# The norms' sums, spread and last stores of a one-core encoder trunk, rearranged

## The chip, the core and the metric

The kernel runs on one core of one Trainium2 chip. Such a core has five engines with a queue of instructions each: TensorE (PE, matrix products; its weight loads are listed as PEld), VectorE (DVE), ScalarE (ACT), GpSimd (POOL) and SyncE (SP), which here issues the DMA transfers. The metric is the device time of one execution, in microseconds (us). The kernel before the change was timed three times, and one more execution was profiled.

## The reference

One layer of a hybrid encoder on 2048 positions of width 1024, in float32, closed by a norm:

```python
def rmsnorm(x, w):
    xf = x.astype(jnp.float32)
    y = xf * lax.rsqrt(jnp.mean(xf * xf, axis=-1, keepdims=True) + EPS)
    return (y * w.astype(jnp.float32)).astype(x.dtype)

def hybrid_layer(x, ...):
    h = rmsnorm(x, norm_mix_w)
    proj = jnp.einsum("btd,dc->btc", h, w_in)
    u_b, u_c, u_h, z, xbc, dt_raw = jnp.split(proj, SPLITS, axis=-1)
    y_a = short_conv_mixer(u_b, u_c, u_h, short_conv_w)
    y_b = ssd_mixer(z, xbc, dt_raw, ssd_conv_w, ssd_conv_b, dt_bias, a_log, d_skip, ssd_norm_w)
    y = jnp.concatenate([y_a, y_b], axis=-1)
    x = x + jnp.einsum("btc,cd->btd", y, w_out)
    h = rmsnorm(x, norm_mlp_w)
    hid = jnp.square(jax.nn.relu(jnp.einsum("btd,df->btf", h, w_up)))
    return x + jnp.einsum("btf,fd->btd", hid, w_down)
...
    return rmsnorm(x, final_norm_w)
```

What matters here is `rmsnorm`: a sum of squares over the 1024 features of each position, a root, and a scaling of all features of that position by its result.

## The kernel before

Activations lie transposed: the 1024 features are eight tiles of 128 partitions, and positions run along the free dimension, in blocks of 512 (`TB`). So a sum over features is a sum over eight tiles and over the 128 partitions. Large products are made of three products of split operands (a high and a low fp32r part each, `mm3`, lines 112 to 114, and the chain at lines 269 to 271). Positions are worked through in two halves of two blocks; the half's two blocks share products in a scheme of seven instead of eight.

The class `Rstd` makes a norm in steps. The eight squares (ScalarE) are added into one tile, `acc`, on VectorE. `reduce` sums that tile over the partitions on PE: with 128 positions at a time as the stationary operand and a column of ones as the moving one, so that `pst` holds a position on each partition and a column for each 128 of them (line 131, fp32). `root` takes the root on ScalarE (line 143) and the reciprocal on VectorE (144), splits the result into two fp32r parts (146, 147), and multiplies the identity by each (`diag`, line 151). `spread` multiplies a matrix of ones by the two diagonal tiles (line 177, fp32r), which puts each position's factor on all partitions, in `prb`; ScalarE copies that to SBUF (line 180). `reduce`, `root` and `spread` serve the first two blocks' norms (`begin_block`, lines 471 to 474), at the very start of the program, where PE has nothing else to do for the first of them, and the three parts of the last norm. The norms between use other functions of the class (`parts`, `whole`), which the change leaves alone.

The program's end is `rest` (line 1025 on): the last products of the second MLP product for the second half, a few features (d) at a time, added to what was accumulated, and with each finished tile its square. It goes through three parts: the third block of 512 positions whole, then the last block in two parts of 256. Each part's norm (`norm_out`, a generator) is advanced by `step()` once ahead of every tile's products of the part that follows, and to its end after the last part. The last square of a part isn't added to `acc` on VectorE: `reduce` sums it on PE beside `acc` (two products per column). Then each of the eight tiles is scaled by its weight and by the factor: five on VectorE in one instruction that reads `prb` (line 1084), three (k = 1, 4, 7) on ScalarE by the weight (1081) and then on GpSimd by the copied factor (1082). SyncE stores each tile (line 1087).

The order on each engine's queue is not the written one throughout: a scheduler places the instructions by the order of writing and its own estimates, and an engine then works through its queue strictly in order.

## Time and profile before

| what | us |
|---|---|
| three runs | 2643.14, 2642.49, 2636.65 |
| their median | 2642.49 |
| the profiled execution's own time | 2640.53 |
| its span, first to last instruction | 2638.80 |
| PE busy | 2588.8 (98%) |
| VectorE busy | 1955.7 (74%) |
| ScalarE busy | 1432.9 (54%) |
| GpSimd busy | 58.2 (2%) |

Times in the profile run from the span's start. A row of the timeline is: start in us, length in us, engine, line, operation, written tile <- read tiles, shapes, the number of instructions (consecutive ones of a kind are merged), and in brackets the idle time of the engine ahead of it with what ended it. A row of the waits is: engine, tile and line that waited, engine, tile and line that ended the wait; the sum in us, the number of times, the longest. An fp32 product shows as two instructions, an fp32r one as one.

### The profile page before, as it was taken

The page shows a single profiled execution, that of the slowest core. Times are in us where ns is not written, and L with a number is a line of the kernel's source. Part 1 is how long each engine was busy: PE and PEld are TensorE (multiplying, and loading weights), DVE is VectorE, ACT ScalarE, POOL GpSimd, SP SyncE. Part 2 cuts the span into 40 slices and gives each one's busy share as a digit, 9 for nine tenths or more (in the row PEclk, how much of TensorE's full clock was granted, in tenths as well). Part 3 has the DMA queues.
Part 4 walks back from the last instruction along what each step waited for, and adds up shares of the span by engine and source line. Part 5 has one row for each costly group of instructions (what it writes and reads, how often), then busy time and mean ns, then how long its engine had stood idle before and what let it go on. Part 6 is the DMA issues. An engine that isn't in the chain of part 4 may idle for free.

```text
span 2638.8 us, 33504 instructions
## 1 busy us (share of the span) xinstructions
PE 2588.8 (98%) x12034; PEld 2127.0 (81%) x12034; DVE 1955.7 (74%) x2696; ACT 1432.9 (54%) x2175; POOL 58.2 (2%) x98
## 2 busy tenths in 40 slices
PE   7999999999999999999999999999999999999998
PEld 5778888788888888888888888788887888888777
DVE  7987676777777777778767765755558877888885
ACT  6644345777667666666326555655555444444443
POOL 0000010000000000000000000000000000000001
PEclk9999999999999999999999999999999999999999
DMA  3585344655555578977665674744448554665762
GB/s 146 190 302 191 137 151 168 207 162 163 171 160 183 154 253 266 283 221 224 211 210 211 232 271 140 261 158 140 161 148 294 165 150 150 214 210 180 238 202 72
DMA packets 283718, 511.25 MB, mean 194 GB/s; under 512 B 25248, under 2 KB 139936, under 8 KB 283552
## 3 DMA queue, kind: packets, MB, share of 16 engines
q1 hardware_dynamic: 283552, 509.12, 58.6%
q8 instruction: 94, 1.54, 0.2%
q14 instruction: 72, 0.59, 0.1%
HBM read 343.88 MB, written 165.15 MB: 193 GB/s over the span
## 4 chain that ended last, share of the span: by engine, by line
PE 65%; issue 25%; DMA 4%; DVE 3%; ACT 3%; SPq 0%; POOL 0%; POOLq 0%; DVEq 0%; ACTq 0%
PE px L269 9%; PE px L271 9%; PE px L270 9%; PE py L269 5%; PE py L271 4%; PE py L270 4%; PE pm L112 4%; PE pm L113 4%; PE pm L114 4%; PE pw L269 2%; PE pw L271 2%; PE pw L270 2%; DMA dec<-rd_d 1%; PE yd L1280 1%; PE yo L1277 1%
## 5 line engine op out<-in xcount | busy, mean ns | idle before, releaser
L269 PE MATMUL px<-uh,whi 128*128 128x512 f32 x1672 | 656.9, 393 | 10.3 <-ACT pw L277 5.6
L271 PE MATMUL px<-uh,wlo 128*128 128x512 f32 x1672 | 651.4, 390 | 2.6 <-DVE wlo L104 2.6
L270 PE MATMUL px<-ul,whi 128*128 128x512 f32 x1672 | 651.9, 390 | 0.0
L269 PEld LDWEIGHTS px<-uh,whi 128*128 128x128 f32 x1672 | 314.1, 188 | 84.7 <-ACT pw L277 8.1
L104 DVE TENSOR_TENSOR wlo<-wraw,whi 128x1024 fp32r<-128x1024 f32 x230 | 233.2, 1014 | 197.9 <-ACT whi L103 197.8
L271 PEld LDWEIGHTS px<-uh,wlo 128*128 128x128 f32 x1672 | 314.3, 188 | 69.5 <-DVE wlo L104 3.4
L270 PEld LDWEIGHTS px<-ul,whi 128*128 128x128 f32 x1672 | 314.4, 188 | 63.8
L103 ACT CAST whi<-wraw 128x1024 fp32r<-128x1024 f32 x230 | 203.5, 885 | 283.3 <-PE px L270 192.1
L103 ACT CAST whi<-s 128x1024 fp32r<-128x1024 f32 x210 | 219.6, 1046 | 233.1 <-PE py L270 76.1
L269 PE MATMUL py<-uh,whi 128*128 128x512 f32 x836 | 326.9, 391 | 2.3 <-DVE acc L986 1.9
L270 PE MATMUL py<-ul,whi 128*128 128x512 f32 x836 | 325.5, 389 | 0.0
L271 PE MATMUL py<-uh,wlo 128*128 128x512 f32 x836 | 325.3, 389 | 0.0
L104 DVE TENSOR_TENSOR wlo<-s,whi 128x1024 fp32r<-128x1024 f32 x210 | 255.2, 1215 | 88.9 <-ACT whi L103 87.0
L112 PE MATMUL pm<-uh,whi 128*128 128x512 f32 (+1 forms) x648 | 252.0, 390 | 2.1 <-ACT uh L204 2.1
L114 PE MATMUL pm<-uh,wlo 128*128 128x512 f32 (+1 forms) x648 | 248.3, 383 | 0.0
L113 PE MATMUL pm<-ul,whi 128*128 128x512 f32 (+1 forms) x648 | 248.3, 383 | 0.0
L269 PEld LDWEIGHTS py<-uh,whi 128*128 128x128 f32 x836 | 156.9, 188 | 35.9 <-DVE acc L986 2.3
L271 PEld LDWEIGHTS py<-uh,wlo 128*128 128x128 f32 x836 | 156.9, 188 | 32.8
L270 PEld LDWEIGHTS py<-ul,whi 128*128 128x128 f32 x836 | 157.0, 188 | 32.2
L269 PE MATMUL pw<-uh,whi 128*128 128x512 f32 x418 | 163.4, 391 | 0.7 <-ACT pw L277 0.7
L319 ACT CAST uh<-rh 128x1024 fp32r<-128x1024 f32 (+1 forms) x128 | 120.4, 944 | 79.1 <-PE py L271 64.4
L271 PE MATMUL pw<-uh,wlo 128*128 128x512 f32 x418 | 162.9, 390 | 0.0
(233 smaller groups left out, 3750.3 us busy)
## 6 DMA issues: line engine op xcount, KB each, us to landing
hid_d<-e SPq DMA_DIRECT2D x96, 512.0 KB, 3.9
rh<-hid_d SPq DMA_DIRECT2D x96, 512.0 KB, 4.4
wraw<-w_in SPq DMA_DIRECT2D x68, 512.0 KB, 4.2
wraw<-w_up SPq DMA_DIRECT2D x64, 512.0 KB, 4.3
wraw<-w_down SPq DMA_DIRECT2D x104, 256.0 KB, 3.7
dec<-rd_d SPq DMA_DIRECT2D x32, 512.0 KB, 5.7
wraw<-w_out SPq DMA_DIRECT2D x32, 512.0 KB, 5.1
x_d<-xt SPq DMA_DIRECT2D x64, 256.0 KB, 3.9
```

The lines of the kernel that those rows point to most:

```text
L103: nc.scalar.copy(hi, raw)
L104: eng.tensor_tensor(out=lo, in0=raw, in1=hi.bitcast(F32), op=ALU.subtract)
L112: nc.tensor.matmul(out, whi, hi, start=(k == 0), stop=False)
L113: nc.tensor.matmul(out, whi, lo, start=False, stop=False)
L114: nc.tensor.matmul(out, wlo, hi, start=False, stop=(k == nk - 1))
L269: nc.tensor.matmul(p, hi, h[0], start=bool(first and k == 0), stop=False, **kw)
L270: nc.tensor.matmul(p, hi, h[1], start=False, stop=False, **kw)
L271: nc.tensor.matmul(p, lo, h[0], start=False, stop=(k == len(g) - 1), **kw)
L319: nc.scalar.copy(p[i][0], t)
L1277: nc.tensor.matmul(yo[:, j * L : (j + 1) * L], state[:, j * P : (j + 1) * P], cT, start=True, stop=True)
L1280: nc.tensor.matmul(yd[(i % 2) * 64 : (i % 2) * 64 + 64, (i // 2) * L : (i // 2 + 1) * L], byhead(t["xdt"])[:, i, :], t["dec"][:, i, :], st ...
```

## The change

Four edits. *The sums:* `reduce` goes through its tiles in the outer loop and through the columns in the inner one. In the last part alone (`final`) the last three squares, not one, are left out of VectorE's sum and given to `reduce`: eight products, the two on `acc` first and the two on the last square at the end. *Root and spread:* the split into two parts is gone, in all norms that use `root`; one diagonal tile in fp32, one fp32 product in place of two fp32r ones. *The scalings:* the tiles of GpSimd are 1, 4 and 5, and ScalarE's scaling by the weight stands right behind the root, ahead of the spread. During the last part's first four tiles `step()` is called twice per tile, and not during its last two. *The stores:* in the last part tiles 1, 3, 4 and 5 are stored by ScalarE's queue, the others by SyncE's.

```diff
--- before.py
+++ after.py
@@ -126,14 +126,15 @@
 
         def reduce(self, *accs):
             pst = psum("tp", "pst", 2)
-            for c in range(self.n):
-                for i, acc in enumerate(accs):
+            for i, acc in enumerate(accs):
+                for c in range(self.n):
                     nc.tensor.matmul(
                         pst[:, c : c + 1],
                         acc[:, c * P : (c + 1) * P],
                         ones[:, 0:1],
-                        start=(i == 0),
+                        start=(i + c == 0),
                         stop=(i == len(accs) - 1),
+                        skip_group_check=True,
                     )
             self.sums = pst[:, 0 : self.n]
 
@@ -142,19 +143,13 @@
             r = self.pool.tile([P, n], F32, tag="rs", name="rs", bufs=2)
             nc.scalar.activation(r, self.sums, AF.Sqrt, bias=eps, scale=self.scale)
             nc.vector.reciprocal(out=r, in_=r)
-            r2 = self.pool.tile([P, 2, n], F32R, tag="rs2", name="rs2", bufs=2)
-            nc.vector.tensor_copy(r2[:, 0, :], r)
-            nc.vector.tensor_tensor(out=r2[:, 1, :], in0=r, in1=r2[:, 0, :].bitcast(F32), op=ALU.subtract)
-            self.diag = []
-            for i in range(2):
-                diag = self.tmp("diag")[:, 0 : self.w].bitcast(F32R)
-                nc.vector.tensor_tensor(
-                    out=diag.rearrange("p (c t) -> p c t", c=n),
-                    in0=ident.unsqueeze(1).to_broadcast([P, n, P]),
-                    in1=r2[:, i, :].bitcast(F32).unsqueeze(2).to_broadcast([P, n, P]),
-                    op=ALU.mult,
-                )
-                self.diag.append(diag)
+            self.diag = self.tmp("diag")[:, 0 : self.w]
+            nc.vector.tensor_tensor(
+                out=self.diag.rearrange("p (c t) -> p c t", c=n),
+                in0=ident.unsqueeze(1).to_broadcast([P, n, P]),
+                in1=r.unsqueeze(2).to_broadcast([P, n, P]),
+                op=ALU.mult,
+            )
 
         def parts(self, acc):
 
@@ -173,8 +168,7 @@
 
         def spread(self, rb=None):
             prb = self.ps = psum("tp", "prb", 2)[:, 0 : self.w]
-            for i in range(2):
-                nc.tensor.matmul(prb, ones_r, self.diag[i], start=(i == 0), stop=(i == 1))
+            nc.tensor.matmul(prb, ones, self.diag, start=True, stop=True)
             if rb is None:
                 rb = self.pool.tile([P, TB], F32, tag="rstd", name="rstd", bufs=1)[:, 0 : self.w]
             nc.scalar.copy(rb, prb)
@@ -1037,6 +1031,7 @@
             sums = [self.dp.tile([P, TB], F32, tag="acc", name="facc", bufs=18) for _ in range(NBB)]
             for bb, t0, w in ((0, 0, TB), (1, 0, TB // 2), (1, TB // 2, TB // 2)):
                 ts = slice(t0, t0 + w)
+                final = t0 > 0
                 st = self.rstd(w)
                 acc = sums[bb][:, ts]
 
@@ -1049,12 +1044,14 @@
 
                 square(0, True)
                 square(4)
+                apart = []
                 for (d, fs, blocks), (whi, wlo) in ws:
                     for i in range(2):
                         at = [(b, j) for b, blk in enumerate(blocks) for j in range(2) if blk == 2 * i + j]
                         if not at:
                             continue
-                        step()
+                        for _ in range(1 + final if d < 3 else 1 - final):
+                            step()
                         pm = psum("mm", "pm", 4)[:, 0:w]
                         todo = [(b * len(fs) + k, j, f) for b, j in at for k, f in enumerate(fs)]
                         for n, (c, j, f) in enumerate(todo):
@@ -1064,27 +1061,36 @@
                             mm3(pm, whi[:, cs], wlo[:, cs], hi, lo, n, len(todo))
                         o = tiles[d + 4 * i, bb][:, ts]
                         nc.vector.tensor_tensor(out=o, in0=pm, in1=o, op=ALU.add)
-                        sq = square(d + 4 * i, False, (d, i) == (3, 1))
-                tails.append(self.norm_out(tiles, bb, ts, st, acc, sq))
+                        alone = (d, i) in (((2, 1), (3, 0), (3, 1)) if final else ((3, 1),))
+                        sq = square(d + 4 * i, False, alone)
+                        if alone:
+                            apart.append(sq)
+                if final:
+                    st.reduce(acc, *apart)
+                tails.append(self.norm_out(tiles, bb, ts, st, final, acc, *apart))
             while tails:
                 step()
 
-        def norm_out(self, tiles, bb, ts, st, *sums):
-            st.reduce(*sums)
+        def norm_out(self, tiles, bb, ts, st, final, *sums):
+            if not final:
+                st.reduce(*sums)
             st.root()
+            slow = (1, 4, 5)
+            for k in slow:
+                nc.scalar.mul(tiles[k, bb][:, ts], tiles[k, bb][:, ts], col(C_NFIN, k))
             yield
             r = st.spread()
             yield
             for k in range(KD):
                 o = tiles[k, bb][:, ts]
-                if k % 3 == 1:
-                    nc.scalar.mul(o, o, col(C_NFIN, k))
+                if k in slow:
                     nc.gpsimd.tensor_tensor(out=o, in0=o, in1=r, op=ALU.mult)
                 else:
                     nc.vector.scalar_tensor_tensor(
                         out=o, in0=o, scalar=col(C_NFIN, k), in1=st.ps, op0=ALU.mult, op1=ALU.mult
                     )
-                nc.sync.dma_start(out[NBB + bb, :, k, ts], o)
+                queue = nc.scalar if final and k in (1, 3, 4, 5) else nc.sync
+                queue.dma_start(out[NBB + bb, :, k, ts], o)
                 if k % 2:
                     yield
```

The line numbers shift: 1047 becomes 1042, 1066 becomes 1063, 1084 becomes 1089, 177 becomes 171. On VectorE, the end of the queue before (sums of squares 1047, tiles picked up from PSUM 1066, scalings of the second part 1084, then the root):

```order
L1066 TENSOR_TENSOR acc<-pm,acc 128x256
L1047 TENSOR_TENSOR facc<-facc,sq 128x256
L1084 SCALAR_TENSOR_TENSOR acc<-acc,cv,prb 128x256
L1047 TENSOR_TENSOR facc<-facc,sq 128x256
L1066 TENSOR_TENSOR acc<-pm,acc 128x256
L1084 SCALAR_TENSOR_TENSOR acc<-acc,cv,prb 128x256
L144 RECIPROCAL rs<-rs 128x2
L146 CAST rs_21862<-rs 128x2
L147 TENSOR_TENSOR rs_21862<-rs,rs_21862 128x2
L151 TENSOR_TENSOR diag<-ident,rs_21862 128x256 x2
L1084 SCALAR_TENSOR_TENSOR acc<-acc,cv,prb 128x256 x5
```

and in the changed program:

```order
L1042 TENSOR_TENSOR facc<-facc,sq 128x256
L1063 TENSOR_TENSOR acc<-pm,acc 128x256
L1089 SCALAR_TENSOR_TENSOR acc<-acc,cv,prb 128x256 x2
L1042 TENSOR_TENSOR facc<-facc,sq 128x256
L1063 TENSOR_TENSOR acc<-pm,acc 128x256 x3
L145 RECIPROCAL rs<-rs 128x2
L147 TENSOR_TENSOR diag<-ident,rs 128x256
L1089 SCALAR_TENSOR_TENSOR acc<-acc,cv,prb 128x256 x5
```

The last three tiles are now picked up one behind the other, with the second part's scalings and all sums of squares ahead of them. On PE, where the second part's norm lies among the last part's products, before:

```order
L114 MATMUL pm<-uh_21439,wlo 128x256
L131 MATMUL pst<-ones_r,facc 128x1
L112 MATMUL pm<-uh_21445,whi 128x256
L113 MATMUL pm<-ul_21446,whi 128x256
L114 MATMUL pm<-uh_21445,wlo 128x256
L112 MATMUL pm<-uh_21451,whi 128x256
L113 MATMUL pm<-ul_21452,whi 128x256
L114 MATMUL pm<-uh_21451,wlo 128x256
L112 MATMUL pm<-uh_20986,whi 128x256
L131 MATMUL pst<-ones_r,sq 128x1
L131 MATMUL pst<-ones_r,facc 128x1
L131 MATMUL pst<-ones_r,sq 128x1
```

and now:

```order
L112 MATMUL pm<-uh_21272,whi 128x256
L131 MATMUL pst<-ones_r,facc 128x1 x2
L113 MATMUL pm<-ul_21273,whi 128x256
L114 MATMUL pm<-uh_21272,wlo 128x256
L112 MATMUL pm<-uh_21427,whi 128x256
L113 MATMUL pm<-ul_21428,whi 128x256
L114 MATMUL pm<-uh_21427,wlo 128x256
L112 MATMUL pm<-uh_21433,whi 128x256
L131 MATMUL pst<-ones_r,sq 128x1 x2
```

Counted in products of 256 columns from the second part's first, `pst` starts after 88 of them (93 before) and `prb` of this norm stands after 104 (118 before, its second product after 120); the first part's `prb` stands after 25 (32 and 35 before). The last part's `pst` and `prb` still follow the last product, number 144. On ScalarE, at the program's start (casts of weights 103, then the first block's copy of `prb` and the second block's first square):

```order
L103 CAST whi<-wraw 128x1024 x2
L180 COPY facc<-prb 128x512
L464 ACTIVATE facc<-x_212 128x512
L204 CAST uh_248<-x_182 128x512
L464 ACTIVATE sq<-x_212 128x512
```

and now:

```order
L103 CAST whi<-wraw 128x1024 x2
L458 ACTIVATE facc<-x_212 128x512
L174 COPY facc<-prb 128x512
L198 CAST uh_242<-x_182 128x512
L198 CAST uh_251<-x_182 128x512
```

The square stands ahead of the copy now. Smaller moves of this kind run through the queues of PE, VectorE, ScalarE and SyncE up to about PE's 800th product; from there to the last parts all queues read as before. At ScalarE's end the four stores are its last instructions, behind the last copy of `prb`.

## The prediction

> **What bounds the kernel now.** I read the page's shares first, then TensorE's waits at both ends of the program, then the timeline of the last 14 us.
>
> ```profile
> PE 2588.8 (98%) x12034; PEld 2127.0 (81%) x12034; DVE 1955.7 (74%) x2696; ACT 1432.9 (54%) x2175; POOL 58.2 (2%) x98
> ```
>
> PE is the bound nearly everywhere, so only three places can pay: the start, where PE has nothing to do, the work added to or taken from PE itself, and the end, after its last large matmul. The waits of PE, first for 0 to 250 us (the first four rows), then from 2400 us on (the last three):
>
> ```profile
> PE pst L131 <- DVE facc L469: 12.9, 1, 12.9
> PE px L271 <- DVE wlo L104: 2.6, 2, 1.5
> PE pm L112 <- ACT uh L204: 2.1, 1, 2.1
> PE prb L177 <- DVE diag L151: 1.6, 1, 1.6
> ...
> PE pst L131 <- DVE facc L1047: 1.6, 1, 1.6
> PE prb L177 <- DVE diag L151: 1.3, 1, 1.3
> PE pst L131 <- ACT sq L1045: 0.5, 1, 0.5
> ```
>
> The edited norm stands in both groups: pst and prb are its two steps on PE. The end, engine by engine:
>
> ```profile
> 2617.96 0.28 PE L114 MATMUL pm<-uh,wlo 128*128 128x256 f32 x1
> 2618.39 0.38 PE L131 MATMUL pst<-ones_r,facc 128*128 128x1 f32 x2
> 2625.69 0.28 PE L113 MATMUL pm<-ul,whi 128*128 128x256 f32 x1
> 2625.81 0.28 PE L114 MATMUL pm<-uh,wlo 128*128 128x256 f32 x1
> 2627.51 0.41 DVE L1066 TENSOR_TENSOR acc<-pm,acc 128x256 f32<-128x256 f32 x1
> 2628.01 0.42 ACT L1045 ACTIVATE sq<-acc 128x256 f32<-128x256 f32 x1 [1.04 <-DVE acc L1066]
> 2628.48 0.38 PE L131 MATMUL pst<-ones_r,sq 128*128 128x1 f32 x2 [0.46 <-ACT sq L1045]
> 2628.95 0.36 PE L131 MATMUL pst<-ones_r,sq 128*128 128x1 f32 x2
> 2629.35 0.26 ACT L143 ACTIVATE rs<-pst,cv 128x2 f32<-128x2 f32 x1 [0.38 <-PE pst L131]
> 2629.64 0.17 DVE L144 RECIPROCAL rs<-rs 128x2 f32<-128x2 f32 x1 [1.34 <-ACT rs L143]
> 2629.84 0.17 DVE L146 CAST rs<-rs 128x2 fp32r<-128x2 f32 x1
> 2630.12 0.75 DVE L151 TENSOR_TENSOR diag<-ident,rs 128x256 fp32r<-128x256 f32 x2
> 2630.59 0.72 PE L177 MATMUL prb<-diag,ones_r 128*128 128x256 f32 x2 [1.28 <-DVE diag L151]
> 2631.81 2.05 DVE L1084 SCALAR_TENSOR_TENSOR acc<-acc,cv,prb 128x256 f32<-128x256 f32 x5 [0.94 <-ACT rstd L180]
> 2631.85 2.09 POOL L1082 TENSOR_TENSOR acc<-acc,rstd 128x256 f32<-128x256 f32 x3 [5.78 <-ACT rstd L180]
> 2632.60 0.33 SPq L1087 DMA_DIRECT2D out<-acc  x1
> 2635.96 0.40 SPq L1087 DMA_DIRECT2D out<-acc  x1
> ```
>
> From PE's last product (done 2626.09) to the span's end at 2638.80 are 12.7 us in three pieces: VectorE picks the product up 1.42 us late, because its queue holds older work; sum, root and spread run from 2627.51 to 2631.81 (call that moment D); then eight stores leave SyncE one by one, the last 2 us after its data were ready (2633.94).
>
> **The change part by part.** *VectorE's backlog.* Of the last part's squares two are no longer added on VectorE (2 x 0.41, by the 256-wide DVE row), and cast, subtraction and one of two diag products go in each norm: 0.17 + 0.16 + 0.65 with four columns, about 0.7 with two. That is some 2.5 us less between the first and last norm, against a backlog of 1.42. In the new order the scalings of the part ahead all stand before the last three pick-ups, which follow each other directly; PE needs six products, 0.12 apart (2625.69 to 2625.81), for each of these tiles, so 0.72, and VectorE 0.41: it has time. Bounds: 0 if other waits keep VectorE late, 1.42 if it is level with PE. I take -1.42, since the work removed is nearly twice the backlog.
>
> *Sums after the last square.* Today three pst products follow it (2628.48 to 2629.31, 0.83 us, one of them on facc). With the order turned, six of eight are done before, and two remain: 0.24 to the second, and 0.36, so 0.60: -0.23.
>
> *Root and spread.* Today reciprocal to the end of prb takes 1.67 (2629.64 to 2631.31). Then: 0.20 to the diag product, 0.47 from its start to prb's (2630.12 to 2630.59), and one fp32 product instead of two fp32r ones. No wide fp32 product of this norm is in the trace; its price comes from these:
>
> ```profile
> 1033.33 1.05 PE L1277 MATMUL yo<-bc,state 128*128 128x128 f32 x8
> 1035.89 0.39 PE L113 MATMUL pm<-ul,whi 128*128 128x512 f32 x1
> 1036.12 0.39 PE L114 MATMUL pm<-uh,wlo 128*128 128x512 f32 x1
> ```
>
> Four fp32 products of 128 columns show as eight instructions; less a drain of 0.16 (0.39 long, 0.23 apart) that is 0.11 each, so 0.22 per 128 columns, 0.44 for 256, 0.89 for 512. An fp32r one of 512 takes 0.23. So the last spread is 0.44 + 0.2 drain = 0.65, the chain 1.32: -0.35 (bounds -0.45 and 0, the latter if an fp32 product cost twice that).
>
> *PE ahead of the end.* The two earlier spreads of the last norm cost 0.89 + 0.44, against two fp32r products each, 0.46 + 0.23: +0.64. Against that stand pauses, such as the 0.31 before the second part's pst (2618.39, where 2618.08 was free), which go if VectorE is less late. Between 0 and +0.64: I take +0.3. So D comes 1.7 earlier against the span's start, if nothing moved there.
>
> *Stores.* Here are all 24 issues (min/median/max ns) and the rate per 1 us slice, 2600 to 2640 us:
>
> ```profile
> L1087 SPq DMA_DIRECT2D out<-acc x24: 332/396/2009, 2613.3 to 2636.0; - x24
> DMA to landing us min/median/max: 1.7/1.9/3.8
> GB/s 0 0 0 0 0 8 0 0 0 0 0 0 0 16 246 6 285 375 381 377 383 53 0 0 0 178 264 264 211 131 0 0 0 150 267 268 269 94 0 0
> ```
>
> The last eight leave D+0.79 to D+4.15, 0.48 apart; 128 KB in 0.48 us is the 267 to 269 GB/s of their slices, while the 256 KB stores of the first part reached 380. So issuing is the limit. With two queues of four, the last tile is ready at D+2.13 (POOL's third), leaves 0.32 later (as the first does after its data) at D+2.45 and lands 1.9 later: D+4.35 against D+6.05, a gain of 1.7. But eight tiles at 380 GB/s need 0.345 each: the first lands at D+2.69, the last then at D+5.1, a gain of 0.95. I take -1.3 between. No DMA is issued by ScalarE in this trace; with the price of SyncE's median 0.40 its four issues fit, with the maximum 2.0 they don't (a rival below). Nothing is queued behind them on ScalarE. The scalings moved ahead of the spread on ScalarE were early already, and cost nothing: ScalarE is idle 1 us and more between the squares.
>
> [...]
>
> *The start.* Both norms of the first stage use the same code:
>
> ```profile
> 15.09 0.18 DVE L144 RECIPROCAL rs<-rs 128x4 f32<-128x4 f32 x1 [1.12 <-ACT rs L143]
> 15.59 1.29 DVE L151 TENSOR_TENSOR diag<-ident,rs 128x512 fp32r<-128x512 f32 x2
> 16.32 1.40 PE L177 MATMUL prb<-diag,ones_r 128*128 128x512 f32 x2 [1.57 <-DVE diag L151]
> 17.76 0.58 ACT L180 COPY facc<-prb 128x512 f32<-128x512 f32 x1 [0.82 <-PE prb L177]
> 18.25 0.63 ACT L464 ACTIVATE facc<-x 128x512 f32<-128x512 f32 x1
> 19.84 1.65 PE L112 MATMUL pm<-uh,whi 128*128 128x512 f32 x3 [2.11 <-ACT uh L204]
> 22.99 0.63 PE L113 MATMUL pm<-ul,whi 128*128 128x512 f32 x1
> 23.41 0.48 PE L114 MATMUL pm<-uh,wlo 128*128 128x512 f32 x1
> ```
>
> Here PE works at half pace: 0.42 apart (22.99 to 23.41) instead of 0.23. The diag product starts 0.20 after the reciprocal, prb 0.73 after that, at 16.03; 0.89 x 0.42/0.23 = 1.63 and a drain of 0.2 end it at 17.9, against 17.72: +0.2. The square that now stands ahead of the copy on ScalarE takes 0.63, and the engine is idle for 0.82 before the copy, so it is hidden if its input has landed. The second norm, on a busy PE, costs 0.89 - 0.46 = +0.43. Sum: +0.6. The order of all engines changes over the first 200 us or so; PE's largest wait there after its first product, 2.6 us for wlo, may shrink or grow. I take 0 for that, between -2 and +2.
>
> **Sum:** -1.42 - 0.23 - 0.35 + 0.3 - 1.3 = -3.0 at the end, +0.6 at the start: -2.4. The profiled execution took 2640.53 (span 2638.80): 2638.1. It lies 0.2 below the mean of the three runs (2640.76), which scatter from 2636.65 to 2643.14; I forecast 2638.4 for the median, the mean less 2.4.
>
> **The rivals.** (1) *The stores gain nothing*, landing as late as before: -1.1, 2639.7. For it: transfers near 380 GB/s; against it: the 267 of today. (2) *PE waits for the moved sums.* In the second part pst stands five products earlier and prb fourteen; if VectorE keeps its backlog, PE stalls there about as long as its present waits by facc and diag at the very end, 1.6 + 1.3 halved, and the 1.42 is not won: -2.4 + 1.45 + 1.42 = +0.5, 2641.2. Against it: the 2.5 us taken from VectorE. (3) *The half pace at the start ends earlier.* It lasts from 19.84 to about 23.4, where a product gets shorter. The longer product at 16.0 keeps PE busy before; were the 3.6 us halved, 1.8 x (1 - 0.23/0.42) = 0.8 would be won; with the start's waits 2 us shorter as well, -5.2: 2635.6. (4) *Slower: ScalarE issues dearly.* Place: the four stores after the last spread. First issue at D+1.06 (POOL's first at D+0.74, and 0.32), last at D+1.06+3c. D is 1.7 earlier, the start 0.6 later, so it is slower than today from 1.06 + 3c = 4.15 + 1.1, c = 1.4 us on. At the maximum of 2.0 the last leaves at D+7.06: +1.8, 2642.6. For it: no row of ScalarE issuing; against it: 0.40 as SyncE's median.
>
> [...]
>
> **How the numbers follow.** Chances: the forecast 0.62, (1) 0.13, (2) 0.12, (3) 0.08, (4) 0.05. All lie within 5.2 us, and 0.3% (about what a measurement of this kernel can tell from no change) is 7.9 us, so only the scatter of runs, 6.5 us wide, can carry the median past it: faster 0.11 (runs like 2636.65 less 2.4 give 2634.25, past 2634.6), same 0.86, slower 0.03. The range goes from the fast run with rival (3)'s half, 2633.5 (2636.65 - 2.4 - 0.8), to the slowest run with rival (2)'s +0.5, 2643.6.
>
> **What would show it.** Right: the last pick-up on VectorE starts within 0.2 us of PE's last product; 0.6 us of pst after the last square; one prb of two rows, 0.65 long; D to the span's end 5.3 to 6.1 instead of 7.0; the first pm product near 20.0. Wrong: store issues on ScalarE of over a microsecond, new waits of PE for facc, sq or diag in the last 20 us, or a first 250 us that shifts by more than 2 us.

## Result and profile after

| | before | after |
|---|---|---|
| median of 16 runs each, us | 2640.18 | 2635.31 |
| ratio of the times, 95% interval | | 0.9982 (0.9975 to 0.9989) |
| profiled execution: own time, us | 2640.53 | 2634.66 |
| its span, us | 2638.80 | 2632.33 |

The kernel is 0.18% faster, 4.9 us by the medians: less than the 0.3% that the prediction took as the limit of what can be told from no change, and twice the 2.4 us forecast. One of the change's 16 runs was a slow one of 3721.07 us, at a granted clock of 0.655; the ratio leaves it out, and without it the median is 2635.02. The spans of the two profiled executions differ by 6.47 us. (The time outside the span is 1.73 us before and 2.33 after, which no stretch shows.) I cut both spans at four moments: the first pm product, the start of the 600th of the px, py and pw products (the input projection, at about 220 us; counted from 0), the first of the 144 pm products that are 256 wide (the last block's two parts), and the end of PE's last large product, T.

| stretch, us | before | after | difference |
|---|---|---|---|
| start to first pm | 19.84 | 19.96 | +0.1 |
| first pm to 600th product | 200.56 | 197.41 | -3.1 |
| 600th product to the last block's parts | 2384.0 | 2383.0 | -1.0 |
| those parts, to T | 21.69 | 21.92 | +0.2 |
| T to the end | 12.71 | 10.02 | -2.7 |

The third row is scatter, as the experiments show. So the end gave nearly what was forecast, -2.5 (the last two rows) where -3.0 was expected, and the first 220 us, forecast at +0.6, came out at -3.0.

PE's share of the page, and its waits, first from 0 to 250 us (four rows), then from 2400 us on (two rows; the two on px, on work that the change leaves alone, are left out):

```profile
PE 2589.8 (98%) x12042; PEld 2128.1 (81%) x12042; DVE 1952.6 (74%) x2679; ACT 1433.9 (54%) x2175; POOL 58.6 (2%) x98
...
PE pst L131 <- DVE facc L463: 12.6, 1, 12.6
PE pm L112 <- ACT uh L198: 2.1, 1, 2.1
PE prb L171 <- DVE diag L147: 1.4, 1, 1.4
PE px L265 <- DVE wlo L104: 1.3, 2, 1.0
...
PE prb L171 <- DVE diag L147: 1.0, 1, 1.0
...
PE pst L131 <- DVE facc L1042: 0.2, 1, 0.2
```

PE's wait of 1.6 for `facc` at the very end is gone: the 0.2 that is left stands at 2614.03, in the second part's norm. The wait for the diagonal went from 1.3 to 1.0, and the one for `wlo` in the first 250 us from 2.6 to 1.3. The timeline of the last 11 us, engine by engine (L1063 picks a product up, L1040 squares, L131 sums, L171 spreads, L1089 scales, L1093 stores):

```profile
2622.03 0.28 PE L114 MATMUL pm<-uh,wlo 128*128 128x256 f32 x1
2622.15 0.50 PE L131 MATMUL pst<-ones_r,facc 128*128 128x1 f32 x4
2622.79 1.50 PE L131 MATMUL pst<-ones_r,sq 128*128 128x1 f32 x12
2625.31 0.70 PE L171 MATMUL prb<-diag,ones_r 128*128 128x256 f32 x2 [1.01 <-DVE diag L147]
...
2621.88 1.07 DVE L1063 TENSOR_TENSOR acc<-pm,acc 128x256 f32<-128x256 f32 x3
2624.62 0.17 DVE L145 RECIPROCAL rs<-rs 128x2 f32<-128x2 f32 x1 [1.67 <-ACT rs L144]
2626.50 2.05 DVE L1089 SCALAR_TENSOR_TENSOR acc<-acc,cv,prb 128x256 f32<-128x256 f32 x5 [1.25 <-ACT rstd L174]
...
2622.32 1.08 ACT L1040 ACTIVATE sq<-acc 128x256 f32<-128x256 f32 x3 [1.03 <-DVE acc L1063]
...
2627.01 2.00 SPq L1093 DMA_DIRECT2D out<-acc  x4
2627.30 2.25 ACTq L1093 DMA_DIRECT2D out<-acc  x4
```

PE's last large product ends at 2622.31 (T). VectorE takes the last three products in a row from 2621.88 on, 0.33 apart, so the last from 2622.54: 0.23 behind PE, where it was 1.42. Of `pst` four instructions on `facc` follow PE's last product directly, and twelve on the squares follow them after 0.14. The spread is one fp32 product of two instructions. The final scalings (D) start at 2626.50, 4.19 after T instead of 5.72, and the span ends 5.83 after D instead of 6.99. For the stores, ScalarE's issues and the rate in slices of 1 us from 2600 to 2640 us:

```profile
L1093 ACTq DMA_DIRECT2D out<-acc x4: 338/380/445, 2627.3 to 2629.1; - x4
GB/s 0 8 0 0 0 0 0 0 0 303 375 377 242 381 334 105 6 0 0 103 267 266 264 148 0 0 0 46 337 335 329 2 0 8 0 0 0 0 0 0
```

The four issues on ScalarE are as short as SyncE's (median 380 ns against 383), and the last eight stores now move at 329 to 337 GB/s in place of 267 to 269. The stores of the part ahead, still on one queue, stand in the same row at 264 to 267.

### The profile page after: what moved, and what is told of

Same layout as the page of the kernel before. It is cut to its first block, busy times and chain, and to the rows that moved or that the text cites. A ratio compares the mean times of both kernels' runs of the same rounds, so it can differ in the third digit from the quotient of the medians.

```text
span 2632.3 us, 33510 instructions
## 1 busy us (share of the span) xinstructions
PE 2589.8 (98%) x12042; PEld 2128.1 (81%) x12042; DVE 1952.6 (74%) x2679; ACT 1433.9 (54%) x2175; POOL 58.6 (2%) x98
## 4 chain that ended last, share of the span: by engine, by line
PE 60%; issue 25%; DMA 6%; DVE 5%; ACT 4%; SPq 1%; POOL 0%; POOLq 0%; DVEq 0%; ACTq 0%
PE px L263 9%; PE px L265 9%; PE px L264 9%; PE py L263 4%; PE py L265 4%; PE py L264 4%; PE pm L112 3%; PE pm L113 3%; PE pm L114 3%; DMA dec<-rd_d 2%; PE pw L263 2%; PE pw L265 2%; PE pw L264 2%; PE yd L1286 1%; ACT dec L1262 1%
## 5 line engine op out<-in xcount | busy, mean ns | idle before, releaser
L104 DVE TENSOR_TENSOR wlo<-wraw,whi 128x1024 fp32r<-128x1024 f32 x230 | 233.1, 1014 | 199.6 <-ACT whi L103 199.4
L103 ACT CAST whi<-s 128x1024 fp32r<-128x1024 f32 x210 | 219.5, 1045 | 225.9 <-PE py L264 81.3
L104 DVE TENSOR_TENSOR wlo<-s,whi 128x1024 fp32r<-128x1024 f32 x210 | 255.3, 1216 | 85.5 <-ACT whi L103 83.9
```

The source lines that it names most:

```text
L103: nc.scalar.copy(hi, raw)
L104: eng.tensor_tensor(out=lo, in0=raw, in1=hi.bitcast(F32), op=ALU.subtract)
```

## The experiments

Twelve runs, each with a profile: ten kernels, and the kernel before and the change once more. Two of the ten, start_only and end_only, were also timed in five rounds. Where a kernel has one time only, it says nothing about half a per mille (the kernel before alone ran from 2632.49 to 2644.04 us in the timed rounds), and the verdict is read from the stretches of its profile.

| kernel | first pm | first pm to 600th | to the parts | parts | T to pick-up | T to sums' end | T to D | D to end | one time |
|---|---|---|---|---|---|---|---|---|---|
| before | 19.84 | 200.56 | 2384.0 | 21.69 | 1.42 | 3.22 | 5.72 | 6.99 | 2640.53 |
| before_again | 19.39 | 200.52 | 2384.6 | 21.68 | 1.44 | 3.24 | 5.94 | 7.01 | 2640.94 |
| end_only | 19.69 | 200.78 | 2373.8 | 21.91 | 0.24 | 1.99 | 4.20 | 5.84 | median 2633.99 |
| after | 19.96 | 197.41 | 2383.0 | 21.92 | 0.23 | 1.98 | 4.19 | 5.83 | 2634.66 |
| after_again | 20.08 | 198.37 | 2384.9 | 21.89 | 0.23 | 1.98 | 4.19 | 5.83 | 2637.64 |
| start_only | 20.20 | 197.99 | 2381.3 | 21.68 | 1.43 | 3.24 | 5.93 | 7.01 | median 2635.1 |
| one_queue | 20.12 | 198.34 | 2376.7 | 21.91 | 0.24 | 1.99 | 4.20 | 7.03 | 2630.28 |
| two_apart | 20.00 | 198.55 | 2379.6 | 21.91 | 0.25 | 2.54 | 5.27 | 5.83 | 2633.54 |
| one_apart | 19.86 | 197.83 | 2381.3 | 21.91 | 0.24 | 2.61 | 5.05 | 5.84 | 2634.17 |
| late_steps | 20.14 | 197.34 | 2382.9 | 21.69 | 0.09 | 1.68 | 3.92 | 5.82 | 2633.99 |
| end_split | 20.12 | 197.24 | 2384.2 | 21.10 | 0.67 | 2.75 | 5.45 | 5.83 | 2636.32 |
| start_dve_back | 22.95 | 200.83 | 2381.5 | 21.67 | 1.43 | 3.85 | 6.54 | 7.01 | 2642.49 |
| start_first | 20.23 | 198.69 | 2383.6 | 21.67 | 1.43 | 3.24 | 5.94 | 7.02 | 2639.08 |
| start_second | 19.65 | 199.29 | 2385.5 | 21.68 | 1.42 | 3.22 | 5.92 | 7.02 | 2640.99 |

All in us, worked out from the starts and lengths of the named instructions in the traces.

**Start alone, end alone.** start_only is the kernel before with the new root and spread in the first two norms (`Whole` holds them):

```diff
+    class Whole(Rstd):
...
-            st = Rstd(self.up, self.tmp, D, TB)
+            st = Whole(self.up, self.tmp, D, TB)
```

> The kernel before, with only the root and spread of the first two norms as in the change (one fp32 diagonal, one fp32 product). The queues of all engines read as in the changed program up to the last norm's parts, and as before from there. Theory A (the new order at the start removes waits of TensorE between 90 and 210 us, which last to the end): the products that lie at 207 us in the kernel before come 2 to 3.5 us earlier, the waits of TensorE from 20 to 250 us sum to about 2 instead of 4.4, the span's end still lies 12.7 us behind the last large product, and the ratio is 0.9988 to 0.9994. Theory B (the 3 us at the start are scatter between executions; the whole lasting gain is the last norm): those products within 1 us of before, ratio 0.9997 to 1.0003.

end_only is the change with the old root and spread there (in `Split`):

```diff
+    class Split(Rstd):
...
-            st = Rstd(self.up, self.tmp, D, TB)
+            st = Split(self.up, self.tmp, D, TB)
```

> The changed kernel, but with the two-part root and spread of before in the first two norms. The queues read as before up to the last norm's parts and as in the changed program from there. Theory A: the products at 207 us within 1 us of before, 10.0 us from the last large product to the span's end (12.7 before), ratio 0.9988 to 0.9992 (2.7 us less 0.3 for the spreads on TensorE). Theory B: the same 10.0 us, but ratio 0.9982 like the whole change.

Measured in the same rounds: start_only 2635.1 us, ratio to the kernel before 0.9994 (0.9985 to 1.0002); end_only 2633.99 us, ratio 0.9986 (0.9975 to 0.9997). The end is faster beyond its interval; the start alone is not told from nothing by its times. The profiles divide more sharply. The tail is 10.03 in end_only and 12.95 in start_only, and the 600th product starts at 218.19 in start_only, like the change, and at 220.47 in end_only, like the kernel before. The queues of VectorE, ScalarE and PE follow the change's order through that stretch in the first case and the old one in the second.

**Does it repeat?** The kernel before and the change, each profiled once more.

> The kernel before, profiled once more. If the profiled times of the start repeat (PE's waits there are set by the order of the queues), the 600th product starts at 220.4 again, within 0.3, and PE's waits from 20 to 250 us sum to 6.5 again. If they scatter like the middle of the program (2373.8 to 2384.0 us from the 600th product to the last block's second part, in six profiled executions), it is off by a microsecond or more, and the comparison of single profiles says nothing about the start. The tail from PE's last large product to the end: 12.7.

> The change, profiled once more: what repeats is the order's, what doesn't is the execution's. From the first pm product to the 600th of the px, py and pw products 197.4 us in the first profile (198.0 to 198.6 in three other kernels with the same order there, 200.5 to 200.8 in three profiles with the order of the kernel before): 197.4 to 198.6. The tail from T to the end 10.0. The middle, from the 600th product to the last block's second part, anywhere from 2373 to 2385.

The start repeats, the middle does not. (before_again missed its expectation in small points: the 600th product starts at 219.91, 0.5 earlier, because its first pm product is 0.45 earlier; and its tail is 12.95, for a reason that stands in the last section.) From the first pm product to the 600th it took 200.52 to 200.78 us in three executions with the old order there, 197.24 to 198.55 in eight with the new one. The middle took 2373.8 to 2385.5 us over all fourteen, without regard to what was changed, so the -1.0 in it is no effect of the change. Averaged over these executions (three and eight), the 600th product starts at 220.26 and at 217.94: the start gives -2.3 rather than the -3.0 of the first two profiles.

**What brings the start's gain?** The gain lies in one stretch, from the 300th to the 600th product. The rows of the busy times by stretch (its bounds, length, then the busy time of PE, PEld, VectorE, ScalarE) for before, before_again, after and after_again:

```profile
146.94:220.40 73.46, 69.56 (x302) 55.92 (x300) 66.07 (x84) 33.74 (x41) 9.77 (x12) 1.00 0.84 299
```

```profile
146.47:219.91 73.44, 69.55 (x302) 55.92 (x301) 66.09 (x84) 33.74 (x41) 10.35 (x12) 1.00 0.85 299
```

```profile
147.21:217.38 70.17, 68.88 (x302) 56.03 (x301) 65.87 (x84) 33.49 (x41) 7.30 (x12) 1.00 0.86 305
```

```profile
148.26:218.45 70.19, 68.90 (x301) 56.02 (x300) 65.89 (x84) 33.49 (x41) 7.32 (x12) 1.00 0.86 306
```

The same 300 products take 3.3 us less, and VectorE does the same 66 us of work in them. Two theories: VectorE comes to the stretch with less backlog since the two norms ask less of it (V), or the scheduler's new order as such does it (O). The test is to give VectorE's work back in start_only, its result unused:

```diff
+            nc.vector.tensor_copy(r2[:, 0, :], r)
+            nc.vector.tensor_tensor(out=r2[:, 1, :], in0=r, in1=r2[:, 0, :].bitcast(F32), op=ALU.subtract)
+            waste = self.tmp("diag")[:, 0 : self.w]
+            nc.vector.tensor_tensor(
+                out=waste.rearrange("p (c t) -> p c t", c=n),
+                in0=ident.unsqueeze(1).to_broadcast([P, n, P]),
+                in1=r2[:, 1, :].bitcast(F32).unsqueeze(2).to_broadcast([P, n, P]),
+                op=ALU.mult,
+            )
             self.diag = self.tmp("diag")[:, 0 : self.w]
```

> The kernel before with the new spread (one fp32 diagonal tile, one fp32 product) in the first two norms, but with VectorE's old work there given back: the cast, the subtraction and a second diagonal product whose result nobody reads. The question is what brought the start's gain: the 600th of the px, py and pw products (the input projection) started at 220.40 us in the kernel before and at 220.47 in the kernel with the old spread there, against 217.38, 218.19, 218.46 and 218.55 in the four that have the new one. Theory V, VectorE's work: from 150 to 200 us VectorE is busy 48.6 of 50 us in the kernel before and PE 46.4, so PE waits for VectorE there, and about 1 us of its work less per norm (0.17 + 0.16 + 0.65) is up to 2 us less ahead of that stretch. By V the 600th product is back at 219.8 to 220.6 and PE's waits from 20 to 250 us sum to 6 or more. Theory O, the order: every engine's queue after the norms is another one, and the gain is that order's luck. By O it lies anywhere from 217 to 222, and the waits with it; 218.6 or less with waits of about 4 would speak for an order that has nothing to do with VectorE's work. First pm product at 20.2 by both.

The row of the same stretch in start_dve_back:

```profile
153.60:223.78 70.18, 68.89 (x302) 56.02 (x301) 65.86 (x84) 33.50 (x41) 7.30 (x12) 1.00 0.86 304
```

70.18, although the work is back. PE comes to this stretch 6 us later here, which could have let VectorE catch up; but in the kernel before VectorE carries no backlog into the stretch either, since it stands idle for 3.31 us at its head (rows below). So V falls for this stretch, and O stands: the order of that kernel departs from the change's in the first two norms, and from some 205 VectorE, 115 ScalarE and 340 PE instructions on, through this stretch, it is the change's again, instruction for instruction. The 600th product comes no earlier all the same (223.78), but for other reasons, which are order too: its first norm ends 3 us later, because VectorE's queue has a weight's low part (L104) ahead of the diagonal products,

```profile
16.17 1.23 DVE L104 TENSOR_TENSOR wlo<-wraw,whi 128x1024 fp32r<-128x1024 f32 x1 [0.35 <-ACT whi L103]
17.31 0.68 DVE L198 TENSOR_TENSOR diag<-ident,rs 128x512 f32<-128x512 f32 x1
17.91 0.68 DVE L205 TENSOR_TENSOR diag<-ident,rs 128x512 f32<-128x512 f32 x1
...
18.65 2.07 PE L214 MATMUL prb<-diag,ones_r 128*128 128x512 f32 x2 [3.75 <-DVE diag L205]
```

and PE waits 2.9 us between 20 and 153 us where it waited for neither before:

```profile
PE px L302 <- ACT pw L310: 1.6, 1, 1.6
PE pc L673 <- DVE dts L666: 1.3, 1, 1.3
```

Of what V expected the sum of the waits held (6.4 from 20 to 250 us), but in other places than V had it, and neither theory had the late first pm. The two norms one by one: each is the kernel before with the new root and spread in one of them (start_first as below, start_second with the condition the other way round):

```diff
-            st = Rstd(self.up, self.tmp, D, TB)
+            st = (Whole if bb == 0 else Rstd)(self.up, self.tmp, D, TB)
```

> The kernel before with the new root and spread in the first norm alone (at 15 us, where VectorE waits for ScalarE and PE for VectorE); the second norm, at 38 us, keeps the two parts. By theory V (less VectorE work) the first norm's saving of VectorE time falls into a stretch in which VectorE has pauses anyway, so little of it can reach the stretch of 150 to 200 us: the 600th product at 219.5 to 220.5. By theory O (the order) it may lie anywhere from 217 to 222. First pm product at 20.0 to 20.2.

> The kernel before with the new root and spread in the second norm alone (at 38 us, VectorE 78% busy there, 97% from 50 us on). By theory V the larger part of the gain stands here: 600th product at 218.0 to 219.5, PE's waits from 20 to 250 us below 5.5. By theory O anywhere from 217 to 222. First pm product as in the kernel before, 19.8.

The stretch from the 300th to the 600th product in start_first, then in start_second:

```profile
147.47:218.92 71.45, 69.46 (x302) 55.92 (x300) 65.82 (x84) 33.62 (x41) 8.32 (x12) 1.00 0.87 307
```

```profile
148.72:218.94 70.22, 68.94 (x302) 56.05 (x301) 65.88 (x84) 33.49 (x41) 7.31 (x12) 1.00 0.86 304
```

The second norm alone brings the change's order there and its whole gain in the stretch (and loses 2.2 us ahead of it, 94.58 us for the first 150 products against 92.18 to 92.37 with the old order); the first alone brings 2.0 of the 3.3. V's number for the second norm held (218.94), its number for the first did not (218.92, expected at 219.5 or later); with VectorE's work back and the gain still there, this is how orders differ, not how a saving of VectorE time adds up. What differs at the stretch's head is to be read on VectorE's queue, before and after (`nb` is a tile of a later norm that is being scaled):

```profile
149.86 0.69 DVE L708 TENSOR_TENSOR buf<-px,s 128x512 f32<-128x512 f32 x1 [3.31 <-PE px L271]
150.47 1.40 DVE L372 SCALAR_TENSOR_TENSOR nb<-nb,cv,facc 128x512 f32<-128x512 f32 x2
```

```profile
147.66 1.47 DVE L366 SCALAR_TENSOR_TENSOR nb<-nb,cv,facc 128x512 f32<-128x512 f32 x2 [0.84 <-DMA nb<-x]
150.13 0.69 DVE L702 TENSOR_TENSOR buf<-px,s 128x512 f32<-128x512 f32 x1 [1.00 <-PE px L265]
```

In the old order VectorE stands idle for 3.31 us behind a product while two scalings are queued behind that wait; in the new one they fill 1.4 us of it. start_dve_back has this head too. But start_first has the old head, and from six VectorE instructions later on the change's order:

```profile
150.39 0.69 DVE L731 TENSOR_TENSOR buf<-px,s 128x512 f32<-128x512 f32 x1 [3.31 <-PE px L294]
151.00 1.41 DVE L395 SCALAR_TENSOR_TENSOR nb<-nb,cv,facc 128x512 f32<-128x512 f32 x2
```

Its stretch is 2.0 shorter than before all the same, and 1.3 longer than the change's. So this swap can account for at most about 1.3 of the 3.3; the rest lies in the order behind it. PE's waits in the stretch sum to 4.0 before, to 1.9 in start_first and to 1.3 in the change. Which other swap shortens them is open; the runs show the order as a whole.

**The stores.** All last stores on SyncE's queue:

```diff
-                queue = nc.scalar if final and k in (1, 3, 4, 5) else nc.sync
+                queue = nc.sync
```

> The changed kernel with all of the last part's stores on SyncE's queue. If issue time limits the stores: from VectorE's first scaling of the last part to the span's end 7.0 us as before, against 5.8 in the changed kernel, and 267 GB/s in the last slices. [...]

D at 4.20 from T, as in the change; D to the end 7.03 in place of 5.83. One queue issues the eight in a single run, 3.78 us long, and the rate (slices of 1 us from 2596 to 2636 us) is the old one:

```profile
2622.04 3.78 SPq L1093 DMA_DIRECT2D out<-acc  x8
...
GB/s 8 0 0 0 0 0 0 20 395 367 248 272 375 391 47 6 0 0 158 266 266 269 89 0 0 0 36 268 266 264 214 0 0 8 0 0 0 0 0 0
```

So the second queue alone is worth 1.2 us, and the limit it lifts is the issue, 0.48 us a store.

**The squares.** Two apart in place of three, and one as in the kernel before:

```diff
-                        alone = (d, i) in (((2, 1), (3, 0), (3, 1)) if final else ((3, 1),))
+                        alone = (d, i) in (((3, 0), (3, 1)) if final else ((3, 1),))
```

> The changed kernel with two squares of the last part given to TensorE instead of three; VectorE adds one more. If TensorE's fp32 sums (0.22 us each) are what follows the last square: the square of the third tile from the end is added by VectorE only after the last pick-up, six products follow that, and the last pst product ends 1.3 us or more behind the last square (0.88 in the changed kernel), D 0.4 later. If two products after the last square were all that counts, as the prediction had it: 0.6 us behind it, D 0.3 earlier than in the changed kernel.

> The change with one square apart in the last part, as in the kernel before, so that two more squares (0.41 us each) are added on VectorE, behind the last pick-ups. With two apart, the sums on PE waited for VectorE's last addition and ended 2.54 us after T instead of 1.98, although the last pick-up stayed level (0.25). By that mechanism one apart costs the two additions, 0.82, behind the last pick-up: the partial sum ready at about T+1.5, four products and a drain of about 1.0: sums end at T+2.5 to T+2.6, 0.5 to 0.6 later than in the change; the pick-up at 0.2 to 0.3. If instead the squares are what made VectorE late (my prediction's view), the pick-up is at 0.6 or more and the sums end at T+2.9 or later.

The pick-up stays level with PE in both (0.25, 0.24): the squares given to PE aren't what made it so. What they buy stands behind it. With two apart, VectorE's queue and the sums, and then with one the additions that follow the last pick-up:

```profile
2619.66 1.07 DVE L1063 TENSOR_TENSOR acc<-pm,acc 128x256 f32<-128x256 f32 x3
2620.66 0.41 DVE L1042 TENSOR_TENSOR facc<-facc,sq 128x256 f32<-128x256 f32 x1
2621.12 0.61 PE L131 MATMUL pst<-ones_r,facc 128*128 128x1 f32 x4 [1.04 <-DVE facc L1042]
```

```profile
2621.47 0.94 DVE L1042 TENSOR_TENSOR facc<-facc,sq 128x256 f32<-128x256 f32 x2
```

An addition on VectorE now follows the last pick-up, PE waits 1.04 for it, and the sums end 2.54 and 2.61 after T instead of 1.98. So the third square apart is worth 0.56, the second 0.07. In two_apart the sums end 1.43 behind the last square, as the first branch of its expectation had it. D is 1.08 later there rather than 0.4: 0.56 by the sums, and 0.52 by the root and spread, for which the clock had fallen (last section). What I expected of one_apart by this mechanism (2.5 to 2.6) held to 0.01; that the squares hold the pick-up up, my prediction's view, did not.

**The steps.** One step of the norm ahead per tile, as in the kernel before:

```diff
-                        for _ in range(1 + final if d < 3 else 1 - final):
+                        for _ in range(1):
```

> The change, but with one step of the norm ahead per tile in the last part, as in the kernel before: two pick-ups, a scaling and the last pick-up then end VectorE's queue, in place of three pick-ups in a row. It tells apart what brought the last pick-up level with PE (0.23 us after PE's last product T, against 1.42 in the kernel before and 0.25 with two squares apart). If the work taken from VectorE did it (my prediction: 2.5 us less against a backlog of 1.42), it stays at 0.2 to 0.3, the tail from T to the end at 10.0. If it is the place of the scalings in the queue, a scaling of 0.41 between two pick-ups whose products come 0.72 apart, the pick-up starts 0.5 to 1.4 after T and the tail is 10.3 to 11.2.

```profile
2621.09 0.74 DVE L1063 TENSOR_TENSOR acc<-pm,acc 128x256 f32<-128x256 f32 x2
2621.76 0.46 DVE L1089 SCALAR_TENSOR_TENSOR acc<-acc,cv,prb 128x256 f32<-128x256 f32 x1
2622.15 0.41 DVE L1063 TENSOR_TENSOR acc<-pm,acc 128x256 f32<-128x256 f32 x1
...
2622.26 1.48 PE L131 MATMUL pst<-ones_r,sq 128*128 128x1 f32 x12
```

Here T is 2622.06. A scaling stands between the last two pick-ups, and the last one still starts 0.09 behind T. A scaling between the pick-ups, my rival, has fallen as the cause: one stands there, and the pick-up is level. Moreover PE waits once in the last 32 us, for the diagonal, where in the change it also waits 0.2 for `facc`; the two narrow parts take 21.69 in place of 21.92 and the tail 9.75 in place of 10.02. By its profile this version is 0.5 us shorter at the end than the change, which its one time can't confirm.

**The spread.** The change with the old root and spread in the last norm alone:

```diff
         def rstd(self, w=TB):
-            return Rstd(self.dp, lambda n: self.raw(n)[:, 0], D, w)
+            return Split(self.dp, lambda n: self.raw(n)[:, 0], D, w)
```

> The change with the old root and spread (two fp32r parts, two diagonal products on VectorE, two products on PE) in the last norm alone. It prices that part: from the last reciprocal to the end of the last spread 1.66 us, as in the kernel before, against 1.38 in the change, or 1.87 if the granted clock falls ahead of the spread, as it did in four kernels that have the old spread. Sums' end at T+2.0, stores 5.84 from D. The tail 10.3, or 10.5. If the one fp32 product brought nothing, the tail stays at 10.0.

```profile
2622.67 1.07 DVE L1093 TENSOR_TENSOR acc<-pm,acc 128x256 f32<-128x256 f32 x3
2623.58 1.83 PE L131 MATMUL pst<-ones_r,sq 128*128 128x1 f32 x12 [0.18 <-ACT sq L1070]
2625.74 0.17 DVE L187 RECIPROCAL rs<-rs 128x2 f32<-128x2 f32 x1 [2.00 <-ACT rs L186]
2626.70 0.92 PE L205 MATMUL prb<-diag,ones_r 128*128 128x256 f32 x2 [1.28 <-DVE diag L194]
```

T is 2622.66, and the last of the three pick-ups starts at 2623.33: 0.67 behind it. Against T the pick-up is 0.44 later than in the change. But T itself is 0.82 earlier here (the parts take 21.10 in place of 21.92), so that from the parts' start the pick-up comes at 21.77, against 22.15 in the change and 23.11 before: it is PE that got ahead, not VectorE that fell behind. Reciprocal to the spread's end is 1.88 (2625.74 to 2627.62) against 1.39 in the change (2624.62 to 2626.01): the dearer case of the expectation. The tail of 11.27 is above both of its numbers, since it left out that the pick-up and the sums would be late too (the run of sums takes 1.83 in place of 1.50, with the clock falling in it). Against that the earlier fp32 spreads and the wait of 0.2 that goes along cost PE 0.8 in the narrow parts. Both together, the change is 0.4 us shorter from the parts' start to the end (31.94 against 32.37). But the fallen clock alone cost this execution an estimated 0.5: 0.33 in the sums (1.83 against 1.50) and 0.21 from the reciprocal to the spread's end (1.88 against 1.67 in the first profile of the kernel before). Without it the two would be level, so this run doesn't show that the new spread gains anything in the last norm.

**What made the pick-up level.** None of the runs on the squares, the steps and the spread brings the 1.42 back. The rows suggest where it came from. In the four kernels of the table below VectorE's last pause ahead of the final pick-up is for the copy of the second part's spread (`rstd`), and from there it works through its queue without another. Before, in the change, and in end_split:

```profile
2623.71 0.87 DVE L1084 SCALAR_TENSOR_TENSOR acc<-acc,cv,prb 128x256 f32<-128x256 f32 x2 [0.15 <-ACT rstd L180]
```

```profile
2618.03 0.48 DVE L1089 SCALAR_TENSOR_TENSOR acc<-acc,cv,prb 128x256 f32<-128x256 f32 x1 [0.77 <-ACT rstd L174]
```

```profile
2619.44 0.48 DVE L1119 SCALAR_TENSOR_TENSOR acc<-acc,cv,prb 128x256 f32<-128x256 f32 x1 [0.29 <-ACT rstd L208]
```

| kernel | second part's spread stands after (products) | that scaling's start, ahead of T | from it to the last pick-up | pick-up after T |
|---|---|---|---|---|
| before | 120 | 2.38 | 3.80 | 1.42 |
| end_split | 113 | 3.22 | 3.89 | 0.67 |
| late_steps | 108 | 3.81 | 3.90 | 0.09 |
| after | 104 | 4.28 | 4.51 | 0.23 |

The work from that scaling to the last pick-up did not shrink, it grew by 0.7. What changed is that the second part's spread stands 16 products earlier, so that VectorE can start on the scalings 1.9 us earlier. The root without the split accounts for 9 of the 16 products (113 to 104); the other 7 come with the rest of the change's edits at the end, which no run takes apart.

## Why the prediction was nearly right, and where not

*The backlog, -1.42.* Measured -1.19 (1.42 to 0.23), about the 0.2 us from PE that I had named. The number held, the mechanism only in part. I had set 2.5 us of work removed from VectorE against a backlog of 1.42. The additions, which I counted in it, bring nothing to the pick-up (one_apart), because the queue puts them behind it. What counted was when the second part's spread let VectorE go on, 4.28 ahead of T in place of 2.38; the root without the split has its share in that by standing ahead of that spread. That the size came out near was partly luck.

*Sums after the last square, -0.23.* Nothing: 0.88 from the last square's end (2628.43) to the last sum's (2629.31) before, 0.89 after (2623.40 to 2624.29). The failed step is "six of eight are done before, and two remain". The three squares come 0.33 apart, by VectorE's and ScalarE's rows of three in 1.07 and 1.08, while PE needs four instructions of 0.11, 0.44, for each. Its run on the squares starts at 2622.79, so at 2623.40 it has done 0.61 of 1.34 and 0.73 are left, with the drain 0.89. With level pick-ups PE itself is the limit; in late_steps, where two squares come earlier, it is 0.73.

*Root and spread, -0.35.* From the reciprocal to D -0.29 (2.17 by 2629.64 and 2631.81 before, 1.88 after), the spread 0.70 long where 0.65 was forecast. It is about 0.2 more against most executions of the old spread, for a reason that I did not foresee (below): in before_again the same step takes 2.37.

*PE ahead of the end, +0.3.* Measured +0.23. Both halves of the sum are to be seen: the two earlier fp32 spreads (+0.64 forecast, 0.6 by end_split's 21.10 against late_steps' 21.69, or 0.8 with the wait of 0.2 in the change), and pauses that went (before takes the same 21.69 with the cheaper spreads). So in the last norm the new spread costs PE ahead of T some 0.6 and gains 0.3 behind it; that it pays there is not shown.

*Stores, -1.3.* Measured -1.16 from D, and one_queue isolates 1.20. What is saved is the time of the issues: on one queue it was larger than the transfer (0.48 a store against some 0.35 for 128 KB, estimated from the 380 GB/s of the larger stores), and it was worth 1.2 us of the end. Rival (1) has fallen, and rival (4) as well: ScalarE's four issues took 0.34 to 0.45.

*The start, +0.6.* This is the step that failed: "The order of all engines changes over the first 200 us or so [...]. I take 0 for that, between -2 and +2." The first norm's price came as said: the longer first spread (2.08, ending at 17.86 against 17.9 forecast), the first pm at 19.96 against 20.0, 20.06 on the mean of eight executions. The second norm's +0.43 can't be read apart from the order. But the new order takes 3.3 us out of the stretch between 147 and 220 us, and the mean over the executions makes the whole start -2.3; with the priced +0.6 taken off, that leaves some -2.9 for the order, outside the bounds. start_dve_back shows how wide such bounds have to be: ahead of the stretch it lost some 3 us twice, in an order that differs in some fifty of VectorE's instructions.

*Rivals (2) and (3).* PE did not wait for the moved sums beyond 0.2. Rival (3), at 2635.6 nearest to the measured 2635.31, had two conditions. The shorter waits came true. The shorter half pace did not: the products get shorter (0.39 us long in place of 0.63) at 22.7 and 25.4 us in the two executions of the change, at 23.4 and 25.1 in the two of the kernel before, which is a matter of the execution. That PE's longer product beforehand ends the half pace sooner is shown by no run. That rival (3) lies so near is luck.

*The sum.* By the profiles that repeat: start -2.3, parts +0.2, tail -2.7 (-2.9 against before_again). That is -4.8 to -5.0, less some 0.4 to 0.6 of longer time outside the span (above), and the medians differ by 4.87. The time stayed inside the stated range because that range was drawn from the scatter of the runs, 10 us wide, and not because the start was understood. The middle's scatter of 11.7 us, which no part of the change touches, is why single times tell nothing here.

## What to carry to other kernels

Where a scheduler orders the queues, an edit's effect on the order can be larger than its own price (here some -2.9 us against +0.6): look for the stretch in which PE waits for an engine that is nearly always busy (here VectorE, 66 of 73 us), and give its reordering wide bounds on both sides. When several small stores close a kernel, compare the interval of issues with the transfer time of one store: here the interval was the longer of the two (0.48 us against some 0.35), and a second queue brought 1.2 us. And a wait that is shortened at one end of a chain (the pick-up, 1.19 us earlier) pays only as far as the next engine (PE's sums) can follow at the new pace: the last sum still ended 0.89 us behind the last square, where 0.60 was forecast.

## What the runs showed of the hardware

The granted clock of PE fell from 1.00 to 0.50 between 1.9 and 5.3 us after the last large product, at a moment that differs from execution to execution (worked out from the rows of five of them, as below), and the spread behind that moment took longer. Rows of 0.8 us (bounds, length, busy times of the engines, the granted clock third from the right) of two_apart with its spread, and of end_split:

```profile
2622.48:2623.28 0.80, 0.14 (x2) 0.06 (x1) 0.29 (x2) 0.26 (x1) 0.00 (x0) 0.65 0.00 0
...
2623.64 1.22 PE L171 MATMUL prb<-diag,ones_r 128*128 128x256 f32 x2 [1.01 <-DVE diag L147]
```

```profile
2624.26:2625.06 0.80, 0.80 (x8) 0.80 (x7) 0.00 (x0) 0.00 (x0) 0.00 (x0) 0.70 0.74 247
```

and of after, where the spread was done by 2626.01:

```profile
2627.11:2627.91 0.80, 0.00 (x0) 0.00 (x0) 0.80 (x3) 0.00 (x0) 0.80 (x2) 0.63 0.06 20
```

If a clock of 1 turns to 0.5 once within the slice, it does so 2.6 us after T in two_apart, 1.9 in end_split and 5.0 in after, by the same reckoning 5.3 in before (0.80 in the slice from 2630.89 to 2631.69) and 3.3 in before_again (0.58 from 2629.37 to 2630.17). The spread takes 1.22 in two_apart, at a granted clock of 0.50, against 0.70 in after, at 1.00. In end_split the clock fell while PE was busy throughout the slice with sums of one column (0.80 of 0.80 us). What makes it fall, and at which moment, no run here tests.

Five executions that have the old spread in the old last norm paid for this: reciprocal to the spread's end was 1.87 in four kernels and in before_again (granted clock 0.50 through its spread), against 1.67 in the first profile of the kernel before, where the fall came only at the spread's end. In after the earlier spread was ahead of the fall, and after_again has the same 4.19 from T to D. That is a gain of about 0.2 us which the profile before, by chance the cheaper case, could not show.
